# One hybrid GLA / SSD / PEER layer: the modulation's matvec in pieces of two weight chunks, summed by a selector matmul

## The chip, the cores and the metric

The kernel runs on one core of one Trainium2 chip. The metric is the device time of one execution in microseconds (us). Before the change, three runs took 3693.89, 3700.24 and 3692.4 us; the median is 3693.89 us.

## The reference, cut to what matters

The layer takes 256 latent tokens `x` and 256 context tokens `ctx`, each with 2048 features, all in float32. Two conditioning vectors, `c` for the latent tokens and `c_ctx` for the context tokens, are turned into the modulation: six shifts, scales and gates of 2048 columns each.

```python
mod_x = jnp.split((jax.nn.silu(c) @ w_ada[layer] + b_ada[layer])[:, None, :], N_MOD, axis=-1)
mod_c = jnp.split((jax.nn.silu(c_ctx) @ w_ada[layer] + b_ada[layer])[None, None, :], N_MOD, axis=-1)
hc = modulate(rmsnorm(ctx, norm1_w[layer]), mod_c[0], mod_c[1])
hx = modulate(rmsnorm(x, norm1_w[layer]), mod_x[0], mod_x[1])
core_c, ctx_states = branch_core(hc, 1, p, None)
core_x, _ = branch_core(hx, rows, p, ctx_states)
x = x + mod_x[2] * branch_out(core_x, p)
hx2 = modulate(rmsnorm(x, norm2_w[layer]), mod_x[3], mod_x[4])
x = x + mod_x[5] * peer(hx2, ...)
return rmsnorm(x, final_norm_w)
```

`w_ada` has 2048 rows and 12288 columns (96 MiB). The change concerns only the product of the two vectors with this matrix; `branch_core` (projections, gated linear attention, state space scan), `branch_out` and `peer` stay as they are.

## The kernel before, in words

**The weight stream.** All large weights pass through one `Stream` (line 29). A chunk is a tile of 128 partitions by 1024 float32 (512 KB). `get()` hands out the next chunk in the order of `plan`; each `get()` first calls `ahead()`, which issues on SP's queue the loads of up to seven chunks ahead and emits the splits of up to three chunks ahead. A split makes two float32r parts of a chunk, `hi` on ACT (line 52) and `lo` on DVE (line 53); modulation chunks are not split, but count among the seven and the three. The tile `raw` has four buffers. During the start, two of three modulation chunks go to five buffers of their own, `raw0`. A load whose buffer still holds a modulation chunk waits until that chunk's matmuls are over.

**The modulation.** `c` and `c_ctx`, after silu, are the first two of 32 columns of `cS`; the other 30 are zero. `ada_piece` (line 248) multiplies one chunk: its 1024 columns are four parts of 256, and four matmuls, one to each group of 32 columns of the array (`tile_position=(0, 32 * g)`, line 253), take one part each. In the start (`halves=1`) the parts are four k-tiles by 256 columns; later (`halves=2`) they are two k-tiles by two halves of 512 columns. Each float32 matmul runs as two passes, so a piece is eight instructions. Four pieces (start) or eight (later) make a block, and the block's partial sums lie in four partition groups of one half of the PSUM bank `ad`. `ada_out` (line 256) is a generator that advances one step at a time: ACT copies the sums to SBUF (line 259), two steps later two PE transposes (line 264) put them on columns, and one step later DVE adds the groups up and adds the bias (lines 270 and 271).

**The start** (lines 365 to 400) follows the list `START` (lines 139 to 150). For each of eight pairs of k-tiles it has eight modulation chunks, four for the scale and four for the shift (16 blocks of 256 columns), and between them the first norm (`norm1`, one step after each piece), the modulated input of the pair before (`h_pair`), and the matmuls of the pair before that (`v_part`, and the small `ld` projection; from the sixth turn on, also half of a key tile `k`). `step()` advances the background generators once after each entry.

**The long projection stage** goes through `units`, 240 further weight chunks with matmuls of 256 or 512 columns (`mm3`, lines 314 to 316; `v_part`, lines 322 to 324), with the scans as background generators. `tick()` comes after each chunk: it advances the generators once and, after every second chunk (`RIDE = 2`), multiplies one modulation chunk with `ride_piece` (line 349). That makes 120 pieces, 15 blocks of 512 columns. For each of eight state space groups the units hold 24 chunks: two xs, four gl, two xs, two C, two xs, two B, two xs and eight z. The eight chunks of the last block (`FILL = 8`) are loaded into tiles `fill` and multiplied later, while PE waits for the second norm (line 1116).

Of the kernel before, what the change touches and what calls it, by code (L numbers as in the profile page):

```python
# [72 lines left out]
class Pairs(list):  # L73
    """tiles of two k-tiles each, read as one"""
# [7 lines left out]
def hybrid_block_kernel(ctx, tc, A, out):  # L82
# [21 lines left out]
    # ------------------------------------------------------------------ plan of the weight stream  # L104
# [3 lines left out]
    W = A["w_f"]                     # feature tiles of w_in: q 0-7, k 8-15, r 16-31, z 32-63, xs 64-95,  # L108
    Q0, K0, R0, Z0, X0, B0, C0, G0 = 0, 8, 16, 32, 64, 96, 104, 112

    # ada chunks (parts after the second) ride along, one with every second chunk of weights
    RIDE, FILL = 2, 8
# [24 lines left out]
    # the start: the parts of the modulation that the first norm needs, 8 chunks to a pair of k-tiles,  # L137
    # with the products of the pair before the last in between, and the first halves of some keys
    START = []
    for c in range(10):  # L140
        todo = [("v", c - 2, 0), ("ld", c - 2, 0), ("v", c - 2, 1), ("ld", c - 2, 1)] if c > 1 else []
        if 4 < c < 9:
            todo.append(("k", c - 5, 0))
        for i in range(8):
            if c < 8:
                START.append(("ada", (8 + c, c)[i // 4], i % 4))
            if i == 3 and 0 < c < 9:
                START.append(("h", c - 1, 0))
            if todo:
                START.append(todo.pop(0))  # L150

    plan = []
    for k, a, b in START:
        if k == "ada":
            plan.append((A["w_ada0"][a, b], False))
# [7 lines left out]
    ride = [(A["w_ada1"][b, i], False) for b in range(16) for i in range(8)]  # L163
    nt = 0
    for u in units:
        for c in unit_chunks(u):
            plan.append(c)
            nt += 1
            if nt % RIDE == 0 and len(ride) > FILL:
                plan.append(ride.pop(0))  # L170
# [20 lines left out]
    # ------------------------------------------------------------------ constants  # L191
# [19 lines left out]
    nc.vector.tensor_scalar(ident, jp, 0.0, None, op0=OP.is_equal)  # L211
    ones = consts.tile([P, P], F32, name="ones")
# [5 lines left out]
    # rows are keys j, columns queries i  # L218
# [28 lines left out]
    # ------------------------------------------------------------------ modulation  # L247
    def ada_piece(i, ps, halves, raw=None):
        """four column groups side by side in the array: four k-tiles by 256 columns, or two by two halves of 512"""
        raw = (st.get() if raw is None else raw).rearrange("p (g n) -> p g n", g=4)  # L250
        nk = 4 // halves
        for g in range(4):
            mm_(ps[32 * g:32 * g + 32, :], cS[:, nk * i + g // halves, :], raw[:, g, :], start=i == 0, stop=i == KT // nk - 1,  # L253
                tile_position=(0, 32 * g), skip_group_check=True)

    def ada_out(b, ps, halves):
        """the sums of a block of 256 or 512 columns, as per-partition columns"""
        sb = xpool.tile([P, 256], F32, name="adasb", tag="adasb", bufs=2)
        nc.scalar.activation(sb, ps, AF.Copy)
        yield  # L260
        yield
        p2 = scbank((P, 2, P))
        for t in range(2):
            nc.tensor.transpose(p2[:, t], sb[:, t * P:(t + 1) * P], ident)
        yield
        p2 = p2.rearrange("p t (j h m) -> p h t m j", h=halves, m=32)
        for h in range(halves):
            n = 2 * (halves * b + h)
            dst = mods[:, :, n:n + 2]
            nc.vector.tensor_reduce(dst.rearrange("p m t -> p t m"), p2[:, h, :, 0:2, :], axis=AX.X, op=OP.add)  # L270
            nc.vector.tensor_add(dst, dst, b_ada[:, None, n:n + 2].to_broadcast([P, 2, 2]))
# [3 lines left out]
    # ------------------------------------------------------------------ norm 1 and the first modulation  # L275
# [33 lines left out]
    def mm3(ps, W2, h0, n, hi, lo, tok, start, stop):  # L309
        """n k-tiles of a feature tile: weights stationary, tokens moving, three float32r passes."""  # L310
# [20 lines left out]
    ride_n, ride_ps = 0, None  # L331
# [10 lines left out]
    def tick(riding=True):  # L342
# [3 lines left out]
        if riding and ticks % RIDE == 0 and ride_n < 128 - FILL:  # L346
            ride_piece()

    def ride_piece(raw=None):
        nonlocal ride_n, ride_ps  # L350
        b, i = divmod(ride_n, 8)
        if i == 0:
            ride_ps = adb[:, b % 2]
        ada_piece(i, ride_ps, 2, raw)
        if i == 7:
            bg.insert(0, ada_out(8 + b, ride_ps, 2))
        ride_n += 1
# [6 lines left out]
    adb = psum.tile([P, 2, 256], F32, name="ad")  # L364
# [4 lines left out]
    for k, a, b in START:  # L369
        if k == "ada":  # L370
            if b == 0:
                ps = adb[:, a // 8]
            ada_piece(b, ps, 1)
            if b == 3:
                bg.append(ada_out(a, ps, 1))
# [39 lines left out]
    # ------------------------------------------------------------------ scratch in DRAM  # L415
# [7 lines left out]
    # ------------------------------------------------------------------ gated linear attention  # L423
# [17 lines left out]
    def decay(hd):  # L441
        """log decays of one head and their running sums, both directions"""
# [37 lines left out]
    def gla(hd):  # L480
# [4 lines left out]
        def exps(d):  # L485
# [5 lines left out]
            # midpoints of both blocks, and the total of the block that comes first  # L491
# [124 lines left out]
    # ------------------------------------------------------------------ state space branch  # L616
# [4 lines left out]
    def dt_stage(pd):  # L621
# [8 lines left out]
        # log1p(u) = 2 atanh(u / (2 + u)), |u / (2 + u)| <= 1/3  # L630
# [50 lines left out]
    def conv(ps, f, nx, o):  # L681
        """depthwise 3x3 over the 4 x 64 grid of latent tokens, and over the 1 x 256 row of context tokens"""
# [20 lines left out]
    def ssd(g):  # L703
        """each step holds what one engine can do while another makes ready the next"""
# [18 lines left out]
        def wide(t, px, row, eng):  # L723
            """token-major columns of eight heads, each times its per-token factor"""
# [25 lines left out]
        # states after the context, one direction to a bank  # L750
# [134 lines left out]
    # ------------------------------------------------------------------ projections, with the scans behind them  # L885
# [52 lines left out]
    # the gated attention's output and the scratch of the out projections, opened when the scans are over  # L938
# [84 lines left out]
    # ------------------------------------------------------------------ out projections and merge  # L1023
# [7 lines left out]
    def gated(n, t, ps):  # L1031
        """t = sum times gate; the next gate is made ready"""
# [39 lines left out]
    def wo_load(i):  # L1072
        """two tiles of the stream, and a chunk for the end of this stage"""
        if i < 8:
            nc.gpsimd.dma_start(x1[:, 2 * i:2 * i + 2], A["xc"][:, 2 * i:2 * i + 2, 0:256])
            if i < FILL:
                fill.append(x1p.tile([P, 1024], F32, name="fill", tag="fill", bufs=FILL))
                nc.gpsimd.dma_start(fill[-1], last_ada[i][0])
# [457 lines left out]
```

## Time and profile before

| what | value |
|---|---|
| median of three runs | 3693.89 us |
| the profiled execution, from first to last instruction | 3694.9 us |
| mean granted TensorE clock | 0.995 |
| PE busy | 3634.8 us, 98% |
| DVE busy | 2221.9 us, 60% |
| ACT busy | 1666.8 us, 45% |
| data moved by DMA | 714.72 MB, mean 193 GB/s |

The profile is one execution. Its span is 1.0 us above the median of the runs; no other time is known of that execution. In the rows below, PE is the matmul side of TensorE and PEld its weight loads, which overlap the matmuls. Consecutive matmuls overlap in time, so what an instruction costs is read from the distance of its start to the next start, not from its duration. A row of the timeline may hold several instructions of one line (x8); its start is that of the first.

### The profile page before, as it was taken

To read this page: it belongs to the slowest core of one execution; us is meant where nothing else is said; L and a number is where in the kernel's file an instruction comes from. 1 tells how busy PE (TensorE), PEld (TensorE's weight loads), DVE (VectorE), ACT (ScalarE), POOL (GpSimd) and SP (SyncE) were. 2 spreads that over 40 slices of the span, in tenths; PEclk is the share of its full clock that TensorE was granted. 3 is DMA by queue.
4 is the path that set the end of the run, shared out by engine and by line. 5 is a ranking of instruction groups with operands and counts; after the bars stand their busy time and mean duration, and the time that the engine had idled before them with its cause. 6 is when DMAs were issued, how large, how long until landed. Compare 5 with 4: busy or idle time off the path is not lost.

```text
span 3694.9 us, 60879 instructions
## 1 busy us (share of the span) xinstructions
PE 3634.8 (98%) x24815; PEld 3196.8 (87%) x24815; DVE 2221.9 (60%) x3401; ACT 1666.8 (45%) x2243; POOL 369.2 (10%) x424
## 2 busy tenths in 40 slices
PE   6999999999999999999999999999999999999998
PEld 3677888888888888899999999999999999998886
DVE  4464344456566656655554688786555555556777
ACT  2253343345454455565443445555444444444444
POOL 0000000000000000011002005462000000000004
PEclk9999999999999999999999999999999999999999
DMA  8554445545654654367657556767556555656764
GB/s 342 210 169 138 145 157 167 186 155 193 194 168 163 202 191 149 127 207 268 196 189 261 169 176 195 207 195 229 196 197 197 199 197 197 199 195 204 242 228 139
DMA packets 196680, 714.72 MB, mean 193 GB/s; under 512 B 22768, under 2 KB 22912, under 8 KB 195888
## 3 DMA queue, kind: packets, MB, share of 16 engines
q1 hardware_dynamic: 171648, 625.03, 50.3%
q0 software_dynamic: 24752, 85.80, 8.3%
q8 instruction: 195, 3.19, 0.4%
q14 instruction: 85, 0.70, 0.1%
HBM read 679.14 MB, written 31.60 MB: 192 GB/s over the span
## 4 chain that ended last, share of the span: by engine, by line
PE 94%; DVE 2%; DMA 1%; issue 1%; ACT 1%; POOL 0%; SPq 0%; DVEq 0%; ACTq 0%; POOLq 0%
PE mm L314 20%; PE mm L316 20%; PE mm L315 20%; PE mm L1454 6%; PE mm L1453 6%; PE mm L1455 6%; PE ad L253 2%; PE mm L322 2%; PE sc L832 2%; PE mm L323 2%; PE mm L324 2%; PE sc L1261 2%; DVE lo L53 1%; PE sc L573 1%; PE sc L765 1%
## 5 line engine op out<-in xcount | busy, mean ns | idle before, releaser
L53 DVE TENSOR_TENSOR lo<-raw,hi 128x1024 fp32r<-128x1024 f32 x996 | 1234.2, 1246 | 1064.5 <-ACT hi L52 1059.4
L52 ACT ACTIVATE hi<-raw 128x1024 fp32r<-128x1024 f32 x996 | 1048.1, 1058 | 1252.5 <-PE mm L315 545.2
L314 PE MATMUL mm<-Hhi,hi 128*128 128x256 f32 (+1 forms) x2272 | 741.3, 326 | 1.8 <-ACT hi L52 1.8
L316 PE MATMUL mm<-Hhi,lo 128*128 128x256 f32 (+1 forms) x2272 | 721.8, 318 | 2.4 <-DVE lo L53 2.4
L315 PE MATMUL mm<-Hlo,hi 128*128 128x256 f32 (+1 forms) x2272 | 720.9, 317 | 0.0
L314 PE MATMUL mm<-h2hi,hi 128*128 128x256 f32 x2304 | 657.7, 285 | 3.3 <-ACT h2hi L1129 3.3
L315 PE MATMUL mm<-h2lo,hi 128*128 128x256 f32 x2304 | 652.9, 283 | 0.0
L316 PE MATMUL mm<-h2hi,lo 128*128 128x256 f32 x2304 | 652.4, 283 | 0.0
L314 PEld LDWEIGHTS mm<-Hhi,hi 128*128 128x128 f32 x2272 | 431.7, 190 | 84.9 <-issue 49.6
L316 PEld LDWEIGHTS mm<-Hhi,lo 128*128 128x128 f32 x2272 | 432.1, 190 | 33.2 <-DVE lo L53 3.5
L315 PEld LDWEIGHTS mm<-Hlo,hi 128*128 128x128 f32 x2272 | 432.4, 190 | 27.8 <-issue 0.5
L314 PEld LDWEIGHTS mm<-h2hi,hi 128*128 128x128 f32 x2304 | 442.3, 192 | 7.0 <-ACT h2hi L1129 3.7
L315 PEld LDWEIGHTS mm<-h2lo,hi 128*128 128x128 f32 x2304 | 442.4, 192 | 3.4 <-DVE h2lo L1132 0.2
L316 PEld LDWEIGHTS mm<-h2hi,lo 128*128 128x128 f32 x2304 | 442.2, 192 | 0.0
L1454 PE MATMUL mm<-lo,ph 128*128 128x512 f32 x1024 | 406.3, 397 | 4.5 <-DVE lo L53 4.5
L1453 PE MATMUL mm<-hi,ph 128*128 128x512 f32 x1024 | 406.6, 397 | 0.0
L1455 PE MATMUL mm<-hi,pl 128*128 128x512 f32 x1024 | 405.3, 396 | 0.0
L1454 PEld LDWEIGHTS mm<-lo,ph 128*128 128x128 f32 x1024 | 193.0, 188 | 48.4 <-DVE lo L53 5.9
L1455 PEld LDWEIGHTS mm<-hi,pl 128*128 128x128 f32 x1024 | 193.1, 189 | 46.9
L1453 PEld LDWEIGHTS mm<-hi,ph 128*128 128x128 f32 x1024 | 193.2, 189 | 43.1
L692 DVE SCALAR_TENSOR_TENSOR s<-mm,convw,s 128x189 f32<-128x189 f32 (+2 forms) x384 | 159.9, 426 | 111.5 <-ACT s L684 107.5
L314 PE MATMUL mm<-yh,hi 128*128 128x256 f32 x768 | 218.2, 284 | 1.0 <-ACT hi L52 1.0
(325 smaller groups left out, 4524.8 us busy)
## 6 DMA issues: line engine op xcount, KB each, us to landing
raw<-in_w_f_dram SPq DMA_DIRECT2D x288, 512.0 KB, 3.8
raw<-in_u_dram SPq DMA_DIRECT2D x256, 512.0 KB, 3.4
raw<-in_v_dram SPq DMA_DIRECT2D x256, 512.0 KB, 4.0
raw<-in_w_ada_dram SPq DMA_DIRECT2D x184, 512.0 KB, 4.4
raw<-in_w_so_dram SPq DMA_DIRECT2D x64, 512.0 KB, 3.4
raw<-in_w_v_dram SPq DMA_DIRECT2D x32, 512.0 KB, 4.1
s<-cum_d POOLq DMA_DIRECT2D x64, 256.0 KB, 6.9
raw<-in_w_ga_dram SPq DMA_DIRECT2D x32, 512.0 KB, 4.7
```

What stands on the lines that cost most here:

```text
L52: self.nc.scalar.activation(hi, t, AF.Copy)
L53: self.nc.vector.tensor_sub(lo, t, hi.bitcast(F32))
L253: mm_(ps[32 * g:32 * g + 32, :], cS[:, nk * i + g // halves, :], raw[:, g, :], start=i == 0, stop=i == KT // nk - 1, tile_position=(0, 32 ...
L314: mm_(ps, Whi[:, j, :], hi[:, k, tok], start=start and j == 0, stop=False)
L315: mm_(ps, Whi[:, j, :], lo[:, k, tok], start=False, stop=False)
L316: mm_(ps, Wlo[:, j, :], hi[:, k, tok], start=False, stop=stop and j == n - 1)
L322: mm_(pv[tb], Hhi[:, k, tok], Whi[:, j, :], start=k == 0, stop=False)
L323: mm_(pv[tb], Hhi[:, k, tok], Wlo[:, j, :], start=False, stop=False)
L692: nc.vector.scalar_tensor_tensor(dst, xi[:, r0 + dr:r1 + dr, c0 + dc:c1 + dc], w[:, t:t + 1], dst, op0=OP.mult, op1=OP.add)
L1453: mm_(ps[t, i], ghi, Whi, start=j == 0 and k == 0, stop=False)
L1454: mm_(ps[t, i], ghi, Wlo, start=False, stop=False)
L1455: mm_(ps[t, i], glo, Whi, start=False, stop=j == 1 and k == 1)
```

## The change

A piece now takes two chunks. Each of the four column groups takes one k-tile by 512 columns, so a matmul has 512 moving columns and a block of 512 columns is four pieces, with the sums in the whole bank `ad`. In the start, the shift and the scale of a pair of k-tiles (256 columns of each) form one block, so there are eight blocks there and not 16; the pieces stand at every second place of the old order. In the projection stage a piece comes after every fourth chunk, and its two chunks lie side by side in the plan. `ada_out` copies 512 columns, then runs four matmuls whose stationary operand is the copied sums (128 by 128) and whose moving operand is `sel2`, two columns that pick and add the four groups; DVE is left with one addition of the bias. The fill is four pieces, at the same place. The layout of `w_ada0` changes on the host to match; comments are also removed.

```diff
-    RIDE, FILL = 2, 8
+    RIDE, FILL = 4, 4
...
-            if c < 8:
-                START.append(("ada", (8 + c, c)[i // 4], i % 4))
+            if c < 8 and i % 2:
+                START.append(("ada", c, i // 2))
...
-            plan.append((A["w_ada0"][a, b], False))
+            plan += [(A["w_ada0"][a, 2 * b + i], False) for i in range(2)]
...
-    ride = [(A["w_ada1"][b, i], False) for b in range(16) for i in range(8)]
+    ride = [[(A["w_ada1"][b, 2 * i + j], False) for j in range(2)] for b in range(16) for i in range(4)]
...
-                plan.append(ride.pop(0))
+                plan += ride.pop(0)
...
+    sel2 = consts.tile([P, 2], F32, name="sel2")
+    nc.vector.tensor_reduce(sel2, ident.rearrange("p (j m) -> p m j", m=32)[:, 0:2, :], axis=AX.X, op=OP.add)
...
-    def ada_piece(i, ps, halves, raw=None):
-        raw = (st.get() if raw is None else raw).rearrange("p (g n) -> p g n", g=4)
-        nk = 4 // halves
+    adb = psum.tile([P, 512], F32, name="ad")
+    def ada_piece(i, raws=None):
+        raws = [(st.get() if raws is None else raws[j]).rearrange("p (k n) -> p k n", k=2) for j in range(2)]
         for g in range(4):
-            mm_(ps[32 * g:32 * g + 32, :], cS[:, nk * i + g // halves, :], raw[:, g, :], start=i == 0, stop=i == KT // nk - 1,
+            mm_(adb[32 * g:32 * g + 32, :], cS[:, 4 * i + g, :], raws[g // 2][:, g % 2, :], start=i == 0, stop=i == 3,
                 tile_position=(0, 32 * g), skip_group_check=True)
...
-        sb = xpool.tile([P, 256], F32, name="adasb", tag="adasb", bufs=2)
-        nc.scalar.activation(sb, ps, AF.Copy)
+        sb = xpool.tile([P, 512], F32, name="adasb", tag="adasb", bufs=1)
+        nc.scalar.activation(sb, adb, AF.Copy)
         yield
         yield
-        p2 = scbank((P, 2, P))
-        for t in range(2):
-            nc.tensor.transpose(p2[:, t], sb[:, t * P:(t + 1) * P], ident)
+        p2 = scbank((P, 4, 2))
+        for t in range(4):
+            mm_(p2[:, t], sb[:, t * P:(t + 1) * P], sel2, start=True, stop=True)
         yield
-        p2 = p2.rearrange("p t (j h m) -> p h t m j", h=halves, m=32)
-        for h in range(halves):
-            n = 2 * (halves * b + h)
-            dst = mods[:, :, n:n + 2]
-            nc.vector.tensor_reduce(dst.rearrange("p m t -> p t m"), p2[:, h, :, 0:2, :], axis=AX.X, op=OP.add)
-            nc.vector.tensor_add(dst, dst, b_ada[:, None, n:n + 2].to_broadcast([P, 2, 2]))
+        if b < 8:
+            dst, bias = (v.rearrange("p m (s n) -> p s m n", s=2)[:, :, :, 2 * b:2 * b + 2]
+                         for v in (mods[:, :, 0:32], b_ada[:, None, 0:32].to_broadcast([P, 2, 32])))
+            nc.vector.tensor_add(dst, p2.rearrange("p (s n) m -> p s m n", s=2), bias)
+        else:
+            n = 4 * b
+            nc.vector.tensor_add(mods[:, :, n:n + 4], p2.rearrange("p t m -> p m t"),
+                                 b_ada[:, None, n:n + 4].to_broadcast([P, 2, 4]))
...
-        if riding and ticks % RIDE == 0 and ride_n < 128 - FILL:
+        if riding and ticks % RIDE == 0 and ride_n < 64 - FILL:
             ride_piece()
...
-            ada_piece(b, ps, 1)
+            ada_piece(b)
             if b == 3:
-                bg.append(ada_out(a, ps, 1))
+                bg.append(ada_out(a))
+            next(n1, None)
             next(n1, None)
...
-    for t in fill:
-        ride_piece(t)
+    for i in range(FILL):
+        ride_piece(fill[2 * i:2 * i + 2])
```

## Rows read from the trace of the kernel before

**Rows 1.** The page: busy us of each engine, share of the span, instructions.

```profile
PE 3634.8 (98%) x24815; PEld 3196.8 (87%) x24815; DVE 2221.9 (60%) x3401; ACT 1666.8 (45%) x2243; POOL 369.2 (10%) x424
```

**Rows 2.** The page: the chain that ended last, by engine.

```profile
PE 94%; DVE 2%; DMA 1%; issue 1%; ACT 1%; POOL 0%; SPq 0%; DVEq 0%; ACTq 0%; POOLq 0%
```

**Rows 3.** Busy time by stage: us, PE, PEld, DVE, ACT, POOL, PEclk, DMA share, GB/s.

```profile
50.00:150.00 100.00, 96.81 (x663) 62.46 (x662) 31.91 (x76) 21.42 (x35) 0.53 (x1) 1.00 0.77 292
...
250.00:1400.00 1150.00, 1148.15 (x7551) 946.28 (x7551) 610.39 (x1032) 519.13 (x866) 50.74 (x78) 1.00 0.52 172
```

**Rows 4.** Line 253, the modulation's matmuls: count, duration ns, first and last start.

```profile
L253 PE MATMUL ad<-raw,cS x1472: 378/379/637, 17.5 to 1399.6; 128*32 128x256 f32 x184
```

**Rows 5.** PE's timeline around one riding piece: start us, us, line, count.

```profile
718.50 0.28 PE L316 MATMUL mm<-Hhi,lo 128*128 128x256 f32 x1
718.71 0.64 PE L253 MATMUL ad<-raw,cS 128*32 128x256 f32 x8
719.28 0.38 PE L314 MATMUL mm<-Hhi,hi 128*128 128x256 f32 x1
719.50 0.28 PE L315 MATMUL mm<-Hlo,hi 128*128 128x256 f32 x1
719.62 0.28 PE L316 MATMUL mm<-Hhi,lo 128*128 128x256 f32 x1
```

**Rows 6.** PE's timeline at the fill: eight pieces in a row, and the next matmul.

```profile
2054.10 3.66 PE L253 MATMUL ad<-fill,cS 128*32 128x256 f32 x64
2061.01 0.58 PE L314 MATMUL mm<-h2hi,hi 128*128 128x256 f32 x1 [3.25 <-ACT h2hi L1129]
```

**Rows 7.** PE's timeline: eight float32 passes of 512 columns on the whole array.

```profile
770.08 3.59 PE L765 MATMUL sc<-s,s 128*128 128x512 f32 x8
773.51 0.27 PE L720 MATMUL sc<-ident,s 128*128 128x128 f32 x1
```

**Rows 8.** PE's timeline around a block's two transposes.

```profile
849.12 0.28 PE L316 MATMUL mm<-Hhi,lo 128*128 128x256 f32 x1
849.24 0.38 PE L264 MATMUL sc<-ident,adasb 128*128 128x128 f32 x2
...
849.57 0.28 PE L315 MATMUL mm<-Hlo,hi 128*128 128x256 f32 x1
```

**Rows 9.** PE's timeline around eight float32 passes with full weights and 128 columns.

```profile
2256.17 0.28 PE L316 MATMUL mm<-h2hi,lo 128*128 128x256 f32 x1
2256.29 1.06 PE L1261 MATMUL sc<-o,o 128*128 128x128 f32 x8
...
2257.30 0.28 PE L315 MATMUL mm<-h2lo,hi 128*128 128x256 f32 x1
```

**Rows 10.** Float32 weight loads of 32 and of 128 columns: busy us, mean ns.

```profile
L253 PEld LDWEIGHTS ad<-raw,cS 128*32 128x32 f32 x1472 | 31.3, 109 | 80.3 <-issue 37.8 <-ACT sq L284 17.4 <-ACT adasb L259 12.0
...
L1261 PEld LDWEIGHTS sc<-o,o 128*128 128x128 f32 x512 | 61.4, 192 | 0.0
```

**Rows 11.** PE's timeline in the start, at the turn from one block to the next.

```profile
59.89 1.93 PE L253 MATMUL ad<-raw,cS 128*32 128x256 f32 x32
62.39 0.64 PE L253 MATMUL ad<-raw,cS 128*32 128x256 f32 x8 [0.56 <-ACT adasb L259]
```

**Rows 12.** DVE's timeline in one state space group.

```profile
955.98 1.22 DVE L53 TENSOR_TENSOR lo<-raw,hi 128x1024 fp32r<-128x1024 f32 x1
957.11 1.22 DVE L814 TENSOR_TENSOR s<-s,s 128x1024 f32<-128x1024 f32 x1
...
961.07 1.22 DVE L53 TENSOR_TENSOR lo<-raw,hi 128x1024 fp32r<-128x1024 f32 x1
```

**Rows 13.** PE's timeline where that group's split chunk is used.

```profile
958.79 0.38 PE L314 MATMUL mm<-Hhi,hi 128*128 128x256 f32 x1
...
959.13 0.28 PE L316 MATMUL mm<-Hhi,lo 128*128 128x256 f32 x1
```

**Rows 14.** What SP's load queue waited for: us in total, times, longest us.

```profile
SPq L44 <- PE ad L253: 456.6, 130, 13.7
```

More of the change, by code (lines that the diff above doesn't have):

```diff
@@ L245, in hybrid_block_kernel, with ada_out @@
     nc.scalar.preload_act_table_set(NLE)
-    def ada_piece(i, ps, halves, raw=None):
-        raw = (st.get() if raw is None else raw).rearrange("p (g n) -> p g n", g=4)
-        nk = 4 // halves
+    adb = psum.tile([P, 512], F32, name="ad")
+    def ada_piece(i, raws=None):
+        raws = [(st.get() if raws is None else raws[j]).rearrange("p (k n) -> p k n", k=2) for j in range(2)]
         for g in range(4):
-            mm_(ps[32 * g:32 * g + 32, :], cS[:, nk * i + g // halves, :], raw[:, g, :], start=i == 0, stop=i == KT // nk - 1,
+            mm_(adb[32 * g:32 * g + 32, :], cS[:, 4 * i + g, :], raws[g // 2][:, g % 2, :], start=i == 0, stop=i == 3,
                 tile_position=(0, 32 * g), skip_group_check=True)
-    def ada_out(b, ps, halves):
-        sb = xpool.tile([P, 256], F32, name="adasb", tag="adasb", bufs=2)
-        nc.scalar.activation(sb, ps, AF.Copy)
+    def ada_out(b):
+        sb = xpool.tile([P, 512], F32, name="adasb", tag="adasb", bufs=1)
+        nc.scalar.activation(sb, adb, AF.Copy)
         yield
         yield
-        p2 = scbank((P, 2, P))
-        for t in range(2):
-            nc.tensor.transpose(p2[:, t], sb[:, t * P:(t + 1) * P], ident)
+        p2 = scbank((P, 4, 2))
+        for t in range(4):
+            mm_(p2[:, t], sb[:, t * P:(t + 1) * P], sel2, start=True, stop=True)
         yield
-        p2 = p2.rearrange("p t (j h m) -> p h t m j", h=halves, m=32)
-        for h in range(halves):
-            n = 2 * (halves * b + h)
-            dst = mods[:, :, n:n + 2]
-            nc.vector.tensor_reduce(dst.rearrange("p m t -> p t m"), p2[:, h, :, 0:2, :], axis=AX.X, op=OP.add)
-            nc.vector.tensor_add(dst, dst, b_ada[:, None, n:n + 2].to_broadcast([P, 2, 2]))
+        if b < 8:
[6 more added lines that the diff above has]
+                                 b_ada[:, None, n:n + 4].to_broadcast([P, 2, 4]))
         ended.add(("ada", b))
@@ L330, in hybrid_block_kernel @@
     ticks = 0
-    ride_n, ride_ps = 0, None
+    ride_n = 0
     def step():
@@ L345, in tick, with ride_piece @@
         ticks += 1
-        if riding and ticks % RIDE == 0 and ride_n < 128 - FILL:
+        if riding and ticks % RIDE == 0 and ride_n < 64 - FILL:
             ride_piece()
[L349 to L356, printed above, removed]
+    def ride_piece(raws=None):
+        nonlocal ride_n
+        b, i = divmod(ride_n, 4)
+        ada_piece(i, raws)
+        if i == 3:
+            bg.insert(0, ada_out(8 + b))
         ride_n += 1
@@ L363, in hybrid_block_kernel @@
     XT, CT = slice(0, 256), slice(0, 512)
-    adb = psum.tile([P, 2, 256], F32, name="ad")
     pv0 = [mmbank() for _ in range(4)]
@@ L370, in hybrid_block_kernel @@
         if k == "ada":
-            if b == 0:
-                ps = adb[:, a // 8]
-            ada_piece(b, ps, 1)
+            ada_piece(b)
             if b == 3:
-                bg.append(ada_out(a, ps, 1))
+                bg.append(ada_out(a))
+            next(n1, None)
             next(n1, None)
@@ L1075, in wo_load @@
             nc.gpsimd.dma_start(x1[:, 2 * i:2 * i + 2], A["xc"][:, 2 * i:2 * i + 2, 0:256])
-            if i < FILL:
-                fill.append(x1p.tile([P, 1024], F32, name="fill", tag="fill", bufs=FILL))
-                nc.gpsimd.dma_start(fill[-1], last_ada[i][0])
+            if i < 2 * FILL:
+                fill.append(x1p.tile([P, 1024], F32, name="fill", tag="fill", bufs=2 * FILL))
+                nc.gpsimd.dma_start(fill[-1], last_ada[i // 2][i % 2][0])
     wo_load(0)
@@ L1483, in _layouts @@
     w = I["w_ada"][0]
-    L["w_ada0"] = f(w[:, :2 * D].reshape(4, 4, P, 16, 256).transpose(3, 0, 2, 1, 4)).reshape(16, 4, P, 1024)
+    L["w_ada0"] = f(w[:, :2 * D].reshape(8, 2, P, 2, 8, 256).transpose(4, 0, 2, 1, 3, 5)).reshape(8, 8, P, 1024)
     L["w_ada1"] = f(w[:, 2 * D:].reshape(8, 2, P, 16, 512).transpose(3, 0, 2, 1, 4)).reshape(16, 8, P, 1024)
```

## The prediction

> **What bounds the kernel now.** I read the page first. PE is busy for 98% of the span, DVE for 60% and ACT for 45% [rows 1], and 94% of the chain that ended last is PE's [rows 2]: time goes down where PE has less to do, and up where PE has to wait. Then the stages. In the long projection stage, from 250 to 1400 us, PE is busy for 1148 of 1150 us while DVE and ACT are about half idle and DMA has a share of 0.52; in the start, from 50 to 150 us, PE is busy for 96.8 of 100 us, and DMA has 0.77 [rows 3]. So both places that the change touches are PE's; only before 50 us does PE wait for loads and for the first norm, and what the change does there I count as nothing, because that wait covers it. TensorE's granted clock is 1.00 in both stages [rows 3], that is its upper level, so durations from there can be used as they stand.
>
> **What a piece costs today.** The modulation has 1472 matmul passes in the stream, eight for each of 184 chunks [rows 4]. Around one riding piece, the last projection matmul before it starts at 718.50 and the second one after it at 719.50: 1.00 us where two steps of 0.12 us (719.50 to 719.62) would stand without the piece. A piece takes 0.76 us of PE [rows 5]. How much of it is streaming? On the whole array, eight float32 passes of 512 columns take 3.43 us, 0.43 us each [rows 7], so one of 256 columns streams for 0.215 us. Eight of these in four column groups at once are 0.43 us; eight pieces in a row take 3.66 us, or 0.46 us each with the entry and the end [rows 6]. So the four groups overlap fully, and a piece that stands alone pays 0.76 - 0.43 = 0.33 us for going into the column groups and out again. That is paid once for each run of pieces, not for each piece.
>
> **The change, step by step.**
>
> *Riding pieces.* 120 pieces of 0.76 us become 60. The new one streams 8 passes of 512 columns, 0.86 us with four groups at once, plus the same 0.33: 1.19 us. The saving is 60 x (1.52 - 1.19) = 19.8 us, all on PE's path.
>
> *The selector.* A block's two transposes cost 0.45 - 0.24 = 0.21 us [rows 8]. In their place stand four float32 matmuls, eight passes, each with its own load of 128 columns and only two moving columns. No row has such a short matmul. The nearest are eight passes with loads of 128 columns and 128 moving columns: 1.13 - 0.24 = 0.89 us, 0.11 us a pass [rows 9]. From below, weight loads of 32 and 128 columns take 109 and 192 ns [rows 10], 83 ns for 96 columns, so 128 columns occupy the load path for about 0.11 us (an estimate from these rows), and a shorter matmul gains nothing. From above, each pass waits for its whole load: 8 x 0.192 = 1.54 us. I take 0.89, since loads run ahead of matmuls in rows 9 too. That is +0.68 us for each of 16 blocks (15 in the projection stage, one after the fill, where PE is the bound again): +10.9 us.
>
> The Trainium skill (TensorEngine Tiling (Array Packing), Instruction Overhead) says that a matmul of one column takes as long as one of some 60 cycles; if that alone counted, a pass would be 25 ns by an estimate from that page, the selector 0.2 us a block, and the sum below about 15 us lower. Rows 9 and 10 speak for the load as the bound; no run here shows two moving columns.
>
> *The start.* In each of the last six turns with modulation chunks, the pieces form four runs (the first three turns) or five (the others), 27 in all; with pieces at every second place there are three a turn, 18. Nine runs less save 9 x 0.33 = 3.0 us. At the turn from block to block PE waits 0.56 us for ACT's copy of the sums [rows 11]; this happens five times in these turns, and afterwards the twelve matmuls of a `v_part` stand between, which covers a copy of 512 columns: -2.8 us. Seven blocks there get the selector in place of 14 pairs of transposes: 7 x 0.89 - 14 x 0.21 = +3.3 us. Together -2.5 us. The bounds: 0, if the loads cannot follow a faster PE, and -6.
>
> *The splits come later.* This is the cost that no row shows directly. The pair of chunks counts twice in the three chunks that are split ahead. Before, the two weight chunks after a piece were split two weight chunks ahead of their use; now the first is handed to ACT and DVE only one weight chunk ahead, after the scan's work of one more tick, and the second just before the piece. In a state space group, `lo` of the first chunk after a piece runs at 955.98 [rows 12], and the third matmul that uses it starts at 959.13 [rows 13]: a margin of 1.9 us. Put behind the scan's work that follows it (957.11 to 961.07, 3.96 us), it would end at 955.98 + 3.96 + 1.22 = 961.16, 2.0 us late, and PE, with the scans' matmuls in order behind it, would wait. Five of the groups show a margin like this, seven have scans behind their projections. Bounds: 0 (elsewhere the margins are mostly over 4 us, and DVE is idle 47% of this stage, so it can catch up) and 7 x 2.0 = 14 us. I take 3 us, nearer to the margins that most chunks have; below zero nothing, since PE hardly waits in this stage now.
>
> *SP's queue.* Loads wait for buffers that modulation chunks hold: 456.6 us in 130 waits [rows 14], and every later load stands behind them. Now two of four buffers are held until the piece is done. The first load behind the piece then has two weight chunks as its lead, where it had two and a piece of 0.76 us. That is covered by the same margins, and I put it into the bound above.
>
> *At nothing.* The fill streams as many columns as before, and PE waits 3.25 us for ACT after it in any case [rows 6]. The larger copy on ACT and the shorter additions on DVE lie on engines that are half idle; a late copy would be met only four chunks later, by the next block's first piece.
>
> **The sum:** -19.8 + 10.9 - 2.5 + 3.0 = -8.4 us. The profiled execution's span is 3694.9 us, 1.0 above the median of 3693.89, so I set the difference against the median: 3685.5 us, 0.23% less. A measurement of this kernel can tell about 0.2% (7.4 us) from no change, so "same" reaches from 3686.5 to 3701.3 us, and my forecast lies just outside. Its own range is 3676 to 3691 us (stalls of 0 to 8 us, the start from 0 to -6).
>
> **The rivals.**
>
> 1. *Late splits take the gain.* The 2.0 us stall comes in seven groups: -19.8 + 10.9 - 2.5 + 14 = +2.6, 3696.5 us. For it: the margin of 1.9 us is smaller than the DVE work moved in front. Against it: DVE's idle half, and the other chunks' margins. Chance 0.18; it becomes slower by over 0.2% at 2.7 us a group.
> 2. *The selector's loads do not overlap.* 1.54 in place of 0.89 us for 23 blocks: +15, 3700.5 us. For it: nothing here has so short a matmul. Against it: loads overlap in rows 9. Chance 0.08.
> 3. *Four groups of 512 columns overlap less than four of 256*, say threefold: 8 x 0.43 / 3 = 1.14 in place of 0.86 us, for 60 riding pieces and 24 in the start: +24, 3709.5 us, the other side. It decides from about +0.19 us a piece on. Against it: the groups of 256 overlap fully [rows 6, 7], and a longer stream in the same bank is the same traffic in each moment. Chance 0.08. The Trainium skill (TensorE: Matmul & The Clock Gate, Measured speedup vs the span model) has 2.38 for three column groups of 512 columns; by that figure a piece would take 1.08 us and the total would be about 3704 (an estimate). The trace's fourfold overlap speaks against it.
> 4. *The change does not save the passage*: the 0.33 us grows with the columns of a piece rather than with runs. Then +10.9 for the selector, +3.3 for it in the start (the waits there taken as left) and +3 for the splits stay: 3711 us. Eight pieces in one run that pay it once [rows 6] speak against it. Chance 0.05.
> 5. *The selector costs no more than the transposes*, because loads of float32 weights can hide behind shorter matmuls: about 15 us less, 3671 us. Chance 0.06.
>
> **How the numbers follow.** The forecast has 0.55, of which 0.40 lies below 3686.5 and 0.15 above it. Faster: 0.40 + 0.06 = 0.46. Same: 0.15, 0.14 of rival 1 and 0.05 of rival 2, 0.34. Slower: rivals 3 and 4 with the rest of 1 and 2, 0.20. The range from 3674 to 3702 holds the forecast and rivals 1 and 2 at their prices, and leaves out rivals 3 to 5, 0.19 together.
>
> **What would show it.** In the new profile: 60 riding runs of eight passes, with about 1.43 us from the last projection matmul before to the second after (1.19 + 0.24); fill with 32 passes in about 3.66 us; eight selector passes a block in about 0.9 us; in the start 18 runs and no wait of 0.56 us for `adasb`; waits of PE for `hi` and `lo` in the projection stage of some 3 us in total. I am wrong if pieces take over 1.3 us, if a selector block takes under 0.4 or over 1.3 us, or if PE's waits for `lo` come once in each group with 2 us.

## The result and the profile after

The changed kernel takes 3720.64 us (median of four runs, 3718.98 to 3723.0), the kernel before 3695.42 us in the same series. The ratio is 1.0067, with a 95% interval from 1.0054 to 1.0079: 0.67% slower, 25 us. The forecast was 8 us less than before, and its range ended at 3702 us. The profiled execution's span is 3721.2 us, that of the slowest of the four runs, against 3694.9 us before.

The page of the changed kernel, first the busy time of each engine, then the chain that ended last, by engine; they answer to [rows 1] and [rows 2]:

```profile
PE 3636.2 (98%) x24175; PEld 3198.7 (86%) x24175; DVE 2215.0 (60%) x3330; ACT 1671.8 (45%) x2235; POOL 366.7 (10%) x424
...
PE 89%; DVE 4%; DMA 3%; ACT 2%; issue 1%; SPq 0%; DVEq 0%; ACTq 0%; POOLq 0%
```

PE has 640 instructions fewer and is no less busy; and five percentage points of the chain have gone from PE to DVE, ACT and DMA. So PE waits in the new kernel, and part of its work takes longer.

**The pieces and the selector.** PE's timeline around one riding piece (it answers to [rows 5]):

```profile
737.14 0.28 PE L321 MATMUL mm<-Hhi,lo 128*128 128x256 f32 x1
737.35 1.07 PE L256 MATMUL ad<-raw,cS 128*32 128x512 f32 x8
738.35 0.38 PE L319 MATMUL mm<-Hhi,hi 128*128 128x256 f32 x1
738.57 0.28 PE L320 MATMUL mm<-Hlo,hi 128*128 128x256 f32 x1
```

From the last projection matmul before the piece to the second after it: 738.57 - 737.14 = 1.43 us, of which two steps of 0.12 us are the projection's. A piece costs 1.19 us. PE's timeline around one block's selector, which answers to [rows 8], and at the fill, to [rows 6]:

```profile
870.07 0.28 PE L321 MATMUL mm<-Hhi,lo 128*128 128x256 f32 x1
870.19 0.95 PE L267 MATMUL sc<-sel,adasb 128*128 128x2 f32 x8
871.00 0.36 PE L319 MATMUL mm<-Hhi,hi 128*128 128x256 f32 x1
871.20 0.28 PE L320 MATMUL mm<-Hlo,hi 128*128 128x256 f32 x1
...
2080.72 3.64 PE L256 MATMUL ad<-fill,cS 128*32 128x512 f32 x32
2087.63 0.58 PE L319 MATMUL mm<-h2hi,hi 128*128 128x256 f32 x1 [3.27 <-ACT h2hi L1130]
```

The selector costs 871.20 - 870.07 - 0.24 = 0.89 us; the fill takes as long as before.

**The waits.** What PE waited for between 160 and 1450 us (engine and waiting line, releaser: us in total, times, longest us). First the kernel before:

```profile
PE mm L322 <- ACT s L928: 1.9, 1, 1.9
PE mm L314 <- ACT hi L52: 1.8, 1, 1.8
PE mm L316 <- DVE lo L53: 1.4, 3, 0.8
```

And the changed one:

```profile
PE mm L327 <- ACT s L929: 11.1, 3, 4.0
PE mm L321 <- DVE lo L53: 10.0, 7, 1.8
PE mm L319 <- ACT hi L52: 3.9, 1, 3.9
PE sc L735 <- ACT s L911: 3.0, 4, 1.4
PE sc L678 <- DVE s L667: 2.9, 1, 2.9
PE mm L319 <- ACT s L439: 0.3, 1, 0.3
```

5.1 us of waits have become 31.2 us. Of the seven waits of line 321 five are the state space groups' (about 1.7 us each, at 858, 982, 1106, 1229 and 1352 us). Three of the longest, near 285, 426 and 561 us, are for line 929 (928 in the kernel before), ACT's copy of the `r` tiles with silu, which sets a PSUM bank free; before there was one such wait, of 1.9 us. The wait of 3.9 us for `hi`, near 231 us, has grown from 1.8 us.

**What stands in front of that copy.** ACT's timeline in the changed kernel before the first of these waits:

```profile
270.98 0.69 ACT L456 ACTIVATE s<-sc,b_lr 128x512 f32<-128x512 f32 x1 [4.76 <-PE sc L451]
...
272.90 1.99 ACT L52 ACTIVATE hi<-raw 128x1024 fp32r<-128x1024 f32 x2
279.23 1.06 ACT L52 ACTIVATE hi<-raw 128x1024 fp32r<-128x1024 f32 x1 [4.34 <-DMA raw<-in_w_v_dram]
...
283.18 1.28 ACT L929 ACT_TABLE_LOAD   x1
284.47 1.08 ACT L929 ACTIVATE s<-mm 128x512 f32<-128x512 f32 x2
```

Two splits stand behind a scan step that waits 4.76 us for PE; as they are late, their `raw` buffers come free late, so the next load is issued late, and ACT then waits 4.34 us for it to land, with the scan's next steps and the `r` copy queued behind. DVE's two `lo` of these splits, and the load that SP issues when the first of them is done, at 275.20 us:

```profile
273.97 2.36 DVE L53 TENSOR_TENSOR lo<-raw,hi 128x1024 fp32r<-128x1024 f32 x2 [1.52 <-ACT hi L52]
...
275.23 0.33 SPq L44 DMA_DIRECT2D raw<-in_w_v_dram  x1
```

It lands 3.9 us later, at 279.12 us, and ACT's next split starts at 279.23. SP's queue shows the same in its waits: between 150 and 1450 us its longest wait for `lo` to free a buffer was 11.3 us before and is 21.8 us now. And PE's timeline at the end of that chain:

```profile
280.70 0.39 PE L329 MATMUL mm<-hi,Hlo 128*128 128x512 f32 x1
285.12 0.79 PE L327 MATMUL mm<-hi,Hhi 128*128 128x512 f32 x1 [4.04 <-ACT s L929]
285.71 0.63 PE L328 MATMUL mm<-lo,Hhi 128*128 128x512 f32 x1
286.14 0.63 PE L329 MATMUL mm<-hi,Hlo 128*128 128x512 f32 x1
```

After the wait the steps are 0.43 us where they are 0.23 us elsewhere: the lower clock. Two windows of the changed kernel (us; then busy time and instructions of PE, PEld, DVE, ACT and POOL; PEclk; DMA share; GB/s), the first around the end of the second of these waits:

```profile
425.00:431.00 6.00, 4.74 (x11) 3.81 (x12) 0.56 (x1) 3.86 (x6) 0.00 (x0) 0.50 0.63 228
500.00:510.00 10.00, 10.00 (x87) 10.00 (x87) 4.32 (x8) 3.18 (x3) 0.00 (x0) 1.00 0.64 214
```

A granted clock of 0.50 is the level of 1.2 GHz. Windows that start at 230.3, 285.0, 425.0, 561.4 and 858.3 us show it: once at the end of the wait for `hi`, three times at or just behind the end of those for the `r` copy, and once behind a group's wait of 1.7 us. Between 150 and 1450 us, 23 matmuls of 512 columns step at 0.43 and 36 of 256 columns at 0.21 us, which is 23 x 0.198 + 36 x 0.093 = 7.9 us more than at the full clock. The other instructions in these stretches are not in this sum, so it is a lower bound; PE is busy for some 20 us in them, which makes 10 us the most. The kernel before has no such stretch. The Trainium skill (TensorE: Matmul & The Clock Gate, HAM oscillation — how this bites in real kernels) describes this: waits for data between stretches of work put the engine back to its lower clock. The trace agrees that the clock falls behind waits, though not behind each: four of the five group waits of some 1.7 us, and the kernel before's two of 1.8 and 1.9 us, leave it at 1.00.

The account: pieces -19.8, selector +10.9, waits +26.1, lower clock +7.9, start -0.3 (below): +24.8 us, against 26.3 between the two profiled executions, from which the terms are read, and 25.2 between the medians.

### The profile page after: what moved, and what is told of

Same layout as the page of the kernel before. It is cut to its first block, busy times and chain, and to the rows that moved or that the text cites. A ratio compares the mean times of both kernels' runs of the same rounds, so it can differ in the third digit from the quotient of the medians.

```text
span 3721.2 us, 59513 instructions
## 1 busy us (share of the span) xinstructions
PE 3636.2 (98%) x24175; PEld 3198.7 (86%) x24175; DVE 2215.0 (60%) x3330; ACT 1671.8 (45%) x2235; POOL 366.7 (10%) x424
## 4 chain that ended last, share of the span: by engine, by line
PE 89%; DVE 4%; DMA 3%; ACT 2%; issue 1%; SPq 0%; DVEq 0%; ACTq 0%; POOLq 0%
PE mm L319 19%; PE mm L321 19%; PE mm L320 19%; PE mm L1454 6%; PE mm L1455 6%; PE mm L1456 6%; DMA raw<-in_w_f_dram 2%; PE ad L256 2%; DVE lo L53 2%; PE mm L327 2%; PE mm L328 2%; PE sc L1262 2%; PE mm L329 2%; PE sc L833 1%; ACT hi L52 1%
## 5 line engine op out<-in xcount | busy, mean ns | idle before, releaser
L321 PE MATMUL mm<-Hhi,lo 128*128 128x256 f32 (+1 forms) x2272 | 724.2, 319 | 11.0 <-DVE lo L53 10.6
L321 PE MATMUL mm<-yh,lo 128*128 128x256 f32 x768 | 216.9, 282 | 0.8 <-DVE lo L53 0.8
```

Of the source, the lines that this page charges most:

```text
L321: mm_(ps, Wlo[:, j, :], hi[:, k, tok], start=False, stop=stop and j == n - 1)
```

## The experiments

All were run beside the kernel before, whose medians in the four series were 3697.36, 3696.56, 3694.39 and 3696.5 us. Two theories stood at first. Theory A: the pair of modulation chunks uses up two of the three chunks that are split ahead. Theory B: it holds two of the four `raw` buffers, so loads come late. Theory C stood against both: the loss comes with the new instructions, not with the order.

**e1_split_by_weights.** The changed kernel; in the long stage `ahead` counts only weight chunks, so three of these are always split ahead.

```diff
-        while self.ns < min(n, self.cur + self.splits):
+        while self.ns < n and (self.ns < self.cur + self.splits if self.limit is not None else
+                               sum(w for _, w in self.plan[self.cur:self.ns]) < self.splits):
```

> The changed kernel, but after the start the splits run three weight chunks ahead, where modulation chunks in between are not counted; loads and buffers stay as they are. Theory A (the pair of modulation chunks takes two of the three places of the split window, so hi and lo are handed to ACT and DVE too late, behind scan work that waits for PE): PE's idle time between 150 and 1450 us falls from 31.9 us to under 10 us, the three waits of about 4 us for the copy of the r tiles go, and with them the stretches at half clock after them; time 3685 to 3695 us. Rival B (the two modulation chunks hold two of the four raw buffers until their piece, so the loads come too late, whatever the order of the splits): the idle time stays above 20 us and the time above 3710 us. Rival C (the 512-column piece, the selector or the single sum bank cost more than their rows): no change, 3720 us.

3690.88 us, ratio 0.9983 (0.9974 to 0.9992): 30 us less than the change, and 6.5 us below the kernel before. PE's waits between 150 and 1450 us, the first four rows:

```profile
PE sc L679 <- DVE s L668: 3.0, 1, 3.0
PE mm L320 <- ACT hi L52: 2.8, 1, 2.8
PE sc L528 <- DVE s L518: 1.7, 2, 1.4
PE mm L328 <- ACT s L930: 1.4, 1, 1.4
```

The five waits of 1.7 us in the state space groups are gone, and of the three for the silu copy one is left, with 1.4 us. All of PE's waits there come to 10.6 us, where theory A had expected under 10, and one stretch at the lower clock stays, from 236 to 246 us.

**e2_raw_buffers.** The changed kernel; modulation chunks of the long stage go to two buffers of their own. To make room, the scan's small tiles have 18 buffers in place of 22.

```diff
-        if self.side and not self.plan[i][1] and i % 3:
+        if self.side and not self.plan[i][1] and (i % 3 or self.limit is None):
...
-    st.limit = st.side = None
+    st.limit = None
+    st.side = (wk, 2)
...
-    NBUF = {"s1": 10, "s2": 22, "s4": 5}
+    NBUF = {"s1": 10, "s2": 18, "s4": 5}
```

> The changed kernel with two buffers of their own for modulation chunks after the start, so that they hold none of the four raw buffers of the weights; to make room the scratch tiles s2 have 18 buffers in place of 22. The split window is as in the changed kernel. Theory A: most of the loss stays, 3710 to 3722 us, since hi and lo are still handed over late. Rival B: idle time of PE between 150 and 1450 us falls under 10 us and the time to 3685 to 3695 us. Rival C: 3720 us.

3693.67 us, ratio 0.9991 (0.9982 to 1.0). So B's remedy is enough as well, against the expectation of theory A for this run, just as e1 went against that of B. What stays is what A named: PE's waits between 150 and 1450 us, the first three rows:

```profile
PE mm L321 <- DVE lo L53: 7.4, 7, 1.1
PE mm L319 <- ACT hi L52: 2.7, 1, 2.7
PE mm L327 <- ACT s L930: 1.4, 1, 1.4
```

`lo` is still late in the five groups, now by 1.1 us, but the long waits behind ACT are gone: with the loads on time, late splits cost 7 us and not 34. Read with the rows above, A and B are two links of one chain, and cutting either breaks the loop between them (late split, late buffer, late load, later split).

**e4_s2_18.** The changed kernel with only the last line of the diff of e2, its control.

> The changed kernel with 18 in place of 22 buffers for the scratch tiles s2 and nothing else: the control for the run with own buffers for modulation chunks. All theories: within 5 us of the changed kernel if the scratch buffers have slack, 3716 to 3726 us; if it is slower, that much is to be taken off the run it controls.

3723.32 us, ratio 1.0071 (1.0056 to 1.0087): the same as the change. What e2 gained came from its `raw` buffers.

**e3_order_alone.** The kernel before, with its old pieces and transposes, but two modulation chunks side by side in the plan and two old pieces in a row after every fourth chunk.

```diff
-    RIDE, FILL = 2, 8
+    RIDE, FILL = 4, 8
...
-                plan.append(ride.pop(0))
+                plan += [ride.pop(0), ride.pop(0)]
...
             ride_piece()
+            ride_piece()
```

> The kernel before with its own 256-column pieces, transposes and both halves of the sum bank, but with two modulation chunks next to each other in the stream and two pieces in a row after every fourth weight chunk (the start is unchanged). PE's own work falls by 60 passages into the column groups, 20 us. Theories A and B (the order of the stream costs): PE idles some 25 us more between 150 and 1450 us and runs at half clock for some 7 us after the longest waits, so 3700 to 3715 us, slower than before. Rival C (the matvec's new shape costs): no new idle time, 3675 to 3680 us.

3714.35 us, ratio 1.0046 (1.0032 to 1.006). PE's waits between 150 and 1450 us, the first three rows:

```profile
PE mm L322 <- ACT s L929: 11.0, 3, 4.0
PE mm L316 <- DVE lo L53: 6.8, 6, 1.8
PE mm L314 <- ACT hi L52: 5.2, 1, 5.2
```

The same lines wait for the same releasers for nearly the same time: 11.0 and 11.1 us at the silu copy. With no new matmul in the kernel, the order brings the loss. C falls.

**e5_before_pairs_window** is e3 with the window of e1; **e7_before_window** is the kernel before with that window and its old order. Both take the diff of e1.

> The kernel before with its own pieces and transposes, two modulation chunks next to each other and two pieces in a row after every fourth weight chunk (as in the run of the order alone), and the split window counted in weight chunks after the start. If the order's cost is the shortened lookahead (theories A and B, which the two runs that lengthen it both bear out), the idle time and the half clock go as they did there, and the 20 us of saved passages stay: PE idle between 150 and 1450 us about 10 us, time 3676 to 3686 us, below the changed kernel with the same window by the selector's 11 us. If the order costs for another reason, 3705 to 3715 us.

> The kernel before with nothing but the split window counted in weight chunks after the start. If the shortened lookahead by pairs is the cause, there is little to gain here, since PE idles only 5.6 us between 150 and 1450 us: 3690 to 3698 us. If the window is worth 20 us or more in any order, the pair is not the cause: 3670 to 3678 us.

e5: 3684.07 us, ratio 0.9969 (0.9957 to 0.9981). e7: 3700.95 us, ratio 1.0011 (1.0002 to 1.002), 3 us above its range. So the window by itself brings nothing to the old order (PE's waits between 150 and 1450 us even rise, from 6.1 to 9.7 us); it mends the pairs. And pairs of old pieces, with it, are 17 us faster than single ones with it. That is most of what the passage of 0.33 us, saved 60 times, makes (19.8 us). PE's timeline around one pair of old pieces in e5:

```profile
719.84 0.28 PE L317 MATMUL mm<-Hhi,lo 128*128 128x256 f32 x1
720.05 1.07 PE L254 MATMUL ad<-raw,cS 128*32 128x256 f32 x16
721.05 0.39 PE L315 MATMUL mm<-Hhi,hi 128*128 128x256 f32 x1
721.27 0.28 PE L316 MATMUL mm<-Hlo,hi 128*128 128x256 f32 x1
```

Again 1.43 us from the matmul before to the second after, as for one new piece: two old pieces in a row get the whole saving, and the new geometry of a piece adds nothing to it. The window is worth 30 us to e3 (3714.35 to 3684.07), as it is to the change.

**e9_r_copy_at_once.** The changed kernel, where the `r` copy is issued with its unit and not put off by one.

```diff
-            later.append(lambda a=a, pr=pr: r_out(a, pr))
+            r_out(a, pr)
```

> The changed kernel, but the copies of the r tiles (silu on ACT) are emitted right after the unit's last tick, ahead of the split of the chunk three ahead, and not one tick later. Theory A' (ACT takes its queue in order; the copies stand behind a split whose chunk is still on its way, and PE's next unit needs the copies' PSUM banks): the three waits of PE of about 4 us before v_part fall under 1.5 us each, and the stretches at half clock after them go: 3703 to 3709 us. Rival (the late load itself holds PE up, whatever stands behind it): the waits only move to the split's first user, 3716 to 3722 us.

3706.08 us, ratio 1.0029 (1.0018 to 1.0039), 14.6 us less than the change. PE's waits for that copy between 160 and 1450 us:

```profile
PE mm L327 <- ACT s L929: 0.8, 1, 0.8
```

11.1 us of waits are down to 0.8. No matmul of 512 columns runs at the lower clock any more, and 15 of 256 do in place of 36 (1.4 us in place of 7.9). The other waits stay, and the one for `hi` grows from 3.9 to 5.9 us: by waits and clock, half of the 34 us remains. So the copy's place behind a late split is shown to make its own waits and the slow stretches behind them, and no more.

**e8_transposes_window** is e1 with transposes again: four of them for the selector's four matmuls, and DVE's reduction, into a small tile.

```diff
-        p2 = scbank((P, 4, 2))
+        p4 = scbank((P, 4, P))
         for t in range(4):
-            mm_(p2[:, t], sb[:, t * P:(t + 1) * P], sel2, start=True, stop=True)
+            nc.tensor.transpose(p4[:, t], sb[:, t * P:(t + 1) * P], ident)
         yield
+        p2 = xpool.tile([P, 4, 2], F32, name="p2", tag="p2", bufs=2)
+        nc.vector.tensor_reduce(p2, p4.rearrange("p t (j m) -> p t m j", m=32)[:, :, 0:2, :], axis=AX.X, op=OP.add)
```

> The changed kernel with the split window counted in weight chunks after the start, and four transposes and a DVE reduction over the groups in place of the four selector matmuls of a block. By the rows, a block's selector takes 0.89 us and four transposes 4 x 0.109 = 0.44 us: 24 blocks, of which some 23 lie on PE's path, are 10 us less than with the selector: 3679 to 3683 us. If the selector hides beside something, 3689 to 3692 us.

3661.42 us, ratio 0.9913 (0.99 to 0.9927): the fastest of all, 35 us under the kernel before and 18 us below what was expected. The surplus is not where the transposes are. Between 1750 and 1950 us there is no modulation, only matmuls of 256 columns back to back, yet PE runs more of them. That window (columns as above) in the kernel before and then in e8:

```profile
1750.00:1950.00 200.00, 200.00 (x1669) 200.00 (x1668) 100.41 (x93) 80.73 (x86) 3.91 (x8) 1.00 0.59 193
```

```profile
1750.00:1950.00 200.00, 200.00 (x1764) 200.00 (x1763) 104.56 (x99) 86.46 (x91) 8.85 (x15) 1.00 0.69 215
```

1669 matmuls are a step of 120 ns, 1764 one of 113 ns, at the same granted clock. The change, e1 to e5, e7 and e9 step at 119.6 to 120 ns there, so what was compared above stands. One thing sets e8 apart besides the transposes: its small tile, 64 bytes a partition, moves what lies behind it in SBUF, the stationary operands `Hhi` and `Hlo` among them. Theory L puts the surplus down to this, theory T to the transposes.

**e10_tile_in_selector** is e1 with that tile, **e11_tile_in_before** the kernel before with it, **e12_transposes_no_tile** e8 without it.

e10:

```diff
+        ps2, p2 = p2, xpool.tile([P, 4, 2], F32, name="p2", tag="p2", bufs=2)
+        nc.vector.tensor_copy(p2, ps2)
```

e11:

```diff
-            nc.vector.tensor_reduce(dst.rearrange("p m t -> p t m"), p2[:, h, :, 0:2, :], axis=AX.X, op=OP.add)
-            nc.vector.tensor_add(dst, dst, b_ada[:, None, n:n + 2].to_broadcast([P, 2, 2]))
+            p3 = xpool.tile([P, 4, 2], F32, name="p3", tag="p3", bufs=2)[:, 0:2]
+            nc.vector.tensor_reduce(p3, p2[:, h, :, 0:2, :], axis=AX.X, op=OP.add)
+            nc.vector.tensor_add(dst, p3.rearrange("p t m -> p m t"), b_ada[:, None, n:n + 2].to_broadcast([P, 2, 2]))
```

e12 (the two lines run for each half `s` of the four columns, in place of one reduction into the tile and one addition):

```diff
-        p2 = xpool.tile([P, 4, 2], F32, name="p2", tag="p2", bufs=2)
...
+            nc.vector.tensor_reduce(dst.rearrange("p m t -> p t m"), p4[:, 2 * s:2 * s + 2, 0:2, :], axis=AX.X, op=OP.add)
+            nc.vector.tensor_add(dst, dst, b_ada[:, None, n:n + 2].to_broadcast([P, 2, 2]))
```

> e1_split_by_weights with one more small tile: DVE copies the eight selected sums into a tile of its own (128x8, two buffers), as the transposes' kernel has it, before it adds the bias. PE's work is that of e1. Theory L (the extra gain of the transposes' kernel comes with that tile, which moves what lies behind it in SBUF, not with the transposes): the step between 256-column matmuls falls from 120 to under 118 ns, and the kernel takes 3665-3678 us. Theory T (the extra gain belongs to the transposes themselves): 3687-3694 us, steps of 120 ns.

> The kernel before, with the same small tile between the reduction and the addition of the bias; PE's work is unchanged. Theory L: steps under 118 ns in the stages without modulation too, 3672-3685 us. Theory T: 3693-3700 us.

> e8_transposes_window without the extra small tile: the reduction is written into the modulation's own columns and the bias added there, as the kernel before does it. Theory L: 3677-3685 us (the selector's price alone is gone), steps of 120 ns. Theory T: 3658-3668 us as in e8_transposes_window.

e10: 3676.89 us, ratio 0.9954 (0.9938 to 0.9971). e11: 3679.17 us, ratio 0.9961 (0.9947 to 0.9975). e12: 3680.17 us, ratio 0.9963 (0.9949 to 0.9977). All three as theory L has it: a tile that does no work to speak of makes the kernel before 15 us faster. The window from 1750 to 1950 us of e11:

```profile
1750.00:1950.00 200.00, 200.00 (x1697) 200.00 (x1697) 102.47 (x95) 81.96 (x87) 5.15 (x10) 1.00 0.61 196
```

118 ns a step. It also settles the selector without the tile: e12's median is 10.7 us below e1's (7.7 when each is set against the kernel before in its own series; the profiled spans are 13.1 us apart), and 23 blocks at 0.89 - 2 x 0.21 = 0.47 us are 10.8.

**e13_tile_128_bytes** asks which move it takes: e11 with four buffers of the small tile in place of two.

```diff
-            p3 = xpool.tile([P, 4, 2], F32, name="p3", tag="p3", bufs=2)[:, 0:2]
+            p3 = xpool.tile([P, 4, 2], F32, name="p3", tag="p3", bufs=4)[:, 0:2]
```

> e11_tile_in_before with four buffers of the small tile in place of two, so that the activations Hhi and Hlo lie 128 bytes a partition further on than in the kernel before, and not 64. In the kernel before and in the changed one the addresses of Hhi (weights) and of hi and lo (moving data) agree modulo 128 bytes; in e11_tile_in_before and e10_tile_in_selector they differ by 64. Theory M (that relation sets the step of a 256-column matmul): with 128 bytes they agree again, the step is 120 ns and the time 3690-3700 us. Theory N (the tile itself, or any move, brings it): 117 to 118 ns and 3676-3684 us.

3705.3 us, ratio 1.0025 (1.0015 to 1.0035): neither theory. The window of e13:

```profile
1750.00:1950.00 200.00, 200.00 (x1685) 200.00 (x1684) 101.97 (x95) 82.28 (x87) 4.29 (x8) 1.00 0.61 195
```

Here 119 ns; but from 250 to 1400 us the mean distance of the starts of consecutive 512-column matmuls is 232.6 ns, over 2189 of them, where the kernel before has 227.7 and e11 230.2. That alone is 2189 x 4.9 ns = 10.7 us. Over the whole kernel the steps account for both runs. In e13, 14,077 steps from one 256-column matmul to the next at the full clock are 0.45 ns shorter than before in the mean, and 5768 between 512-column ones 2.63 ns longer: -6.35 + 15.15 = +8.8 us, where its span is 9.6 us longer. In e11 they are 2.02 ns shorter and 1.77 ns longer: -28.45 + 10.25 = -18.2 us, where its span is 18.1 us shorter. So N falls, since e11 and e13 differ only in the number of the tile's buffers, and with it in where things lie; and M is too simple, since the step did not go back to that of before. A rule by a longer distance is not excluded: by the programs' addresses `Hhi` and `hi` agree modulo 256 bytes in the kernel before, and not in e13. That placement moves the step is shown; by what rule is open.

## Why the prediction was wrong

*Riding pieces*: right. 1.43 us from matmul to matmul where 1.43 was forecast, so 60 x 0.33 = 19.8 us are saved; e5 against e7 shows 17 of them by itself. Rivals 3 and 4 fall: four groups of 512 columns overlap fully, also at the fill (3.64 us). By the figure of 2.38 for three column groups that the forecast gave from the Trainium skill (TensorE: Matmul & The Clock Gate, Measured speedup vs the span model) a piece would have had to take 1.08 us and the passage, 1.41 us, where 1.19 was measured; the trace does not agree.

*The selector*: right, 0.89 us a block. The 25 ns a pass worked out from the Trainium skill (TensorEngine Tiling (Array Packing), Instruction Overhead) is not what a float32 pass with a load of 128 columns costs: the eight passes take 112 ns each (0.89 / 8). Rivals 2 and 5 fall.

*The start*: forecast -2.5 us, measured near nothing: the same matmul at the end of the start comes 0.3 us earlier than before (at 173 us). The 18 runs and the end of the turn waits came as forecast, but other waits took their place. PE's waits from 60 to 165 us, in the kernel before and in the changed one:

```profile
PE ad L253 <- ACT adasb L259: 2.8, 5, 0.6
```

```profile
PE mm L328 <- DVE lo L53: 2.6, 4, 0.8
```

The kernel before has 1.0 us of waits for splits there, so this takes 1.6 us back. And the stretch before 50 us, counted as nothing, is not quite that: the first matmul of line 323 starts at 47.90 us, the same one (line 328) at 48.78 in the changed kernel.

*The splits come later*, with *SP's queue* inside it: this is the step that failed. Its first half was right: `lo` is 1.7 us late in five groups, as the forecast had it with 2.0 us, and for its reason. DVE's timeline in one of them, and PE's matmul that waits, in the changed kernel:

```profile
854.02 1.29 DVE L817 TENSOR_TENSOR s<-s,s 128x512 f32<-128x512 f32 x2
855.22 0.48 DVE L839 SCALAR_TENSOR_TENSOR s<-s,dskip,sc 128x256 f32<-128x256 f32 x1
...
856.85 1.22 DVE L53 TENSOR_TENSOR lo<-raw,hi 128x1024 fp32r<-128x1024 f32 x1
```

```profile
858.12 0.49 PE L321 MATMUL mm<-Hhi,lo 128*128 128x256 f32 x1 [1.70 <-DVE lo L53]
```

But 3 us were taken and 14 set as the bound, and it came to 34: 26.1 us of waits and at least 7.9 us of the lower clock. Three things were missing.

1. The bound was made from DVE's queue in one stage. ACT's in the stage before was not looked at: there splits share it with scan steps that wait for PE, and with the copy that frees PE's bank. Three waits for that copy are 11.1 us.
2. SP's queue was put inside the bound "by the same margins". It is not a second view of one delay but a further link, which turns a late split into a late load and ACT's wait for it: e2 took the loads out, and 27 us of the loss went.
3. That an idle half of DVE and ACT "can catch up" was the argument for 3 us. In the rows above ACT stood idle for 4.34 us with the scan's steps and the `r` copy queued behind the split: that idle time caught up on nothing.

The lower clock after a wait had no term at all. Rival 1 had the mechanism and its sign, at 3696.5 us, but was priced by the groups alone. Their stall was the 1.7 us shown, under the 2.7 us a group (19 us in all) at which it saw the loss begin; what carried the sum past 19 us were the waits in the stage before and the clock.

## What to carry to other kernels

When an edit changes the order of a stream, find what counts chunks (split places, buffers, loads) and whether a chunk that needs no work takes a place there; two such chunks side by side can use up the whole lookahead, and here a window that counts only chunks with work gave 30 us back. Price a later split on every queue that it shares, by what stands behind it in order, never by that engine's idle share. And before a difference under half a per cent is put down to an edit, compare the step of matmuls that the edit did not touch: a tile that moves others in SBUF can shift it.

## What the runs showed that had not been expected

A new tile of 64 bytes a partition, with PE's work unchanged, moved this kernel by -15 us (e11), and one of 128 bytes by +9 us (e13): as much as the whole change was meant to bring. Steps of 256-column matmuls from 113 to 120 ns and of 512-column ones from 227 to 234 ns were seen at a granted clock of 1.00; the kernel before has both 227.7 ns (250 to 1400 us) and 233.0 ns (2500 to 3300 us). The rule behind it, and why e8 alone reached 113 ns in one stage, stays open. The Trainium skill (TensorE: Matmul & The Clock Gate, Back-to-back issue gap) gives, for the gap between isolated matmuls, 2.5 ns on top of the columns at 2.4 GHz, by which an estimate for 256 columns is 109 ns; no kernel here reached it, and e8's 113 comes nearest.
